# A two-block model on one core: another order of the mixer's branches, three jobs at a time, and other durations in the emission clock

## The chip, the core and the metric

The kernel runs on one core of a Trainium2 chip. The metric is device time in microseconds (us) of one execution, as the median of several runs. On the core, TensorE (PE) does matrix products, VectorE (DVE), ScalarE (ACT) and GpSimd (POOL) do elementwise work, and SyncE (SP) issues most DMAs. Each engine takes its instructions strictly in the order in which the program issued them, so that an instruction that waits holds up all that stands behind it on its engine.

## The reference

The model has 512 tokens of width 1024. The first block has two layers; each is a mixer, a mixture of experts and a gated per-layer embedding. The second block is an attention with forgetting, a convolutional feed-forward part, an HGRN2 recurrence and a second feed-forward part. The change is in the mixer, which has four branches on the same normed input:

```python
h = rms_norm(x, g_mix[i])
a_q, a_k, a_v, s_z, s_x, s_b, s_c, s_dtf, s_dtb, c_q, c_k, c_v, d_uv = split(h @ w_in[i])
o_a = gqa_block_attention(rope(norm(a_q)), rope(norm(a_k)), a_v)          # branch 0
o_b = bidir_ssd(s_z, s_x, s_b, s_c, s_dtf, s_dtb, ...)                     # branch 1
#     depthwise conv of 5 taps, two state-space scans, times silu(z), rms_norm
o_c = rms_norm(diff_block_attention(c_q, c_k, c_v, lam, rel_bias)) * ...   # branch 2
#     two softmaxes per head, subtracted
o_d = spatial_gating(d_uv, ...)                                           # branch 3
gates = sigmoid(h @ w_branch_gate[i])                                     # 1024 -> 4 * 1024
merged = sum_n gates[n] * (branch_n @ w_branch[i][n])                     # 256 -> 1024 each
x = x + merged @ w_out[i]
```

## The kernel before

Activations lie feature by token: eight tiles of 128 x 512. Dense products are made to float32 accuracy from two halves: a weight piece of 128 x 1024 is split by ScalarE into a high half `ph` (a cast) and by VectorE, every fourth time by GpSimd, into a low half `pl` (a subtraction), and each product is three matmuls (high by high, high by low, low by high). An output tile of 128 x 512 from 1024 inputs is thus a *step* of 24 matmuls; a step of a branch's output product (`w_branch`, 256 inputs) has six.

The mixer (`Net.mixer`) runs two things side by side. The **filler** is a list of such steps (`blocks`): the projections by `w_in`, the 32 gate steps with the 32 branch steps in between (`steps`), and `w_out`. `Runner.go` issues it step by step. After a step's matmuls it issues its *evacuation* (VectorE takes the result from PSUM into a tile `w`); there are two PSUM banks `mm` for it. `PCS` weight pieces (four, with their tiles `ph` and `pl`) may be split and not yet used up, and SyncE loads 1 MB blocks of weights into `RAW` = 2 buffers. The **jobs** are Python generators (`jobs`): the norm, the setup, the decay terms of the state-space branch, and the four branches, `gqa` (branch 0), `sgu` (3), `diff` (2), `ssm` (1). After every six filler matmuls, `Runner.go` may issue one job step: `Jobs.step` looks at the first `window` = 2 jobs of the list and takes the first that is due. A branch's output step waits until its job is done; if that isn't so when its turn comes, job steps are issued one after another with no filler between them.

Whether a job is due, and whether one may be issued at all, is told by a model of the engines' times, `Clock`: `Clock.run` adds for each issued instruction an estimated duration to its engine. A job waits until the clock of TensorE has reached the time at which its last results are there, plus `LAG`; and no job step is issued while the clock of VectorE or ScalarE is more than `slack` = 4 us ahead of that of TensorE. The same clock orders the issue of the later phases `fox` and `hgrn` (with `window` = 1) and of `ple`.

In `steps`, the gates come in the order `[3, 0, 2, 1]`, with the projections `z` and `x` of the state-space branch behind the first eight gate steps. A branch's eight output steps follow its gates four steps later, one after each filler step (`behind`). In `jobs`, `diff` waits for `gqa`, and `ssm` waits for all of `x` and for `diff`. The tiles `w` (2 KB a partition) come from a pool of `WN` = 38. In `ssm`, `start` and `taps` are the convolution (its weights are `cwh`), `fetch` loads rows of decay sums over SyncE's queue (`w<-lrow`), `rows` makes the decay matrix `f` and the weights `u.W` of a head (with `col`), `weights` multiplies them, three products of each head on GpSimd, and `outputs` makes the head's output.

Of the kernel before, what the change touches and what calls it, by code (L numbers as in the profile page):

```python
# [13 lines left out]
F32 = mybir.dt.float32  # L14
# [123 lines left out]
class Clock:  # L138


    LAG = 0.15

    def __init__(self):
        self.t = dict.fromkeys(("tensor", "vector", "scalar", "gpsimd", "sync"), 0.0)
# [6 lines left out]
    def run(self, eng, f, out, ins, accum):  # L151
        start = max([self.t[eng], self.free.pop(out.tensor.name, 0.0)] + [self.done.get(a.tensor.name, 0.0) for a in ins])
        n = max([a.free_size() for a in ins] + [out.free_size()])
        if f == "dma_start":
            self.dma = max(self.dma, start) + out.size() / 90000
            cost, busy = self.dma + 2.0 - start, 0.1
        elif eng == "tensor":
            passes = 2 if f == "transpose" else 4 if ins[-1].dtype == F32 else 1
            cost = busy = 0.0025 + passes * ins[-1].free_size() / 2400 * (0.5 if out.shape[0] <= 64 else 1)
        else:  # L160
            fix, per = {"vector": (0.07, 960), "scalar": (0.1, 1200), "gpsimd": (0.15, 476)}[eng]
            cost = busy = fix + n / per
        self.t[eng] = start + busy
        for a in [out] + accum:
            self.done[a.tensor.name] = start + cost + self.LAG
        for a in [out] + ins:
            self.last[a.tensor.name] = start + cost + self.LAG
        if eng != "tensor":
            self.mark = max(self.mark, start + cost + self.LAG)

# [372 lines left out]
class Net:  # L543
# [246 lines left out]
    def mixer(self, i, X, nxt):  # L790
        nc, I = self.nc, self.I
        w = I["w_in"][i]
# [43 lines left out]
        def steps():  # L836

            behind = deque()
            order = [3, 0, 2, 1]
            src = [("g", order[0]), ("p", proj("z", O_Z, 256, 0.5)), ("p", proj("x", O_X, 768))] + [("g", n) for n in order[1:]]  # L840
            for kind, v in src:
                if kind == "g":
                    behind.extend([None] * max(0, 4 - len(behind)))
                    behind.extend(branch(v, v == order[0], v == order[-1]))
                for st in gates(v) if kind == "g" else v:
                    yield st
                    b = behind.popleft() if behind else None
                    if b is not None:
                        yield b
            yield from (b for b in behind if b is not None)  # L850
# [12 lines left out]
        def blocks():  # L863
            yield from proj("aq", O_AQ, 256, cols=qv)
            yield from proj("akv", O_AK, 256)
            yield from proj("uv", O_U, 512, 0.5)
            yield from proj("cq", O_CQ, 256, -(32.0 ** -0.5))
            yield from proj("ck", O_CK, 256)
            yield from proj("cv", O_CV, 256)
            yield from steps()  # L870
            yield Step([], None, turn_over, ready=lambda: len(ms) == ND)
            yield from self.stream(I["w_out"][i], 0, D, ms, evo)
# [9 lines left out]
        def jobs():  # L882
            yield self.xnorm_job(N)
            if i == 0:
                yield chain((lambda: N.R is not None,), self.setup_job(), self.bias_job())
            yield chain((lambda: "setup" in self.made,), self.decays(i, dtw, xs, N, B))
            yield job(0, lambda: self.gqa(i, pj.pop("aq"), pj["akv"], rope), wait("akv", 2), lambda: "setup" in self.made)
            yield job(3, lambda: self.sgu(i, pj.pop("uv")), wait("uv", 4))
            yield job(2, lambda: self.diff(i, pj.pop("cq") + pj.pop("ck"), pj.pop("cv")), wait("cv", 2), lambda: 0 in out)
            yield job(1, lambda: self.ssm(i, B, wait("x", 6), lambda: (pj.pop("z"), pj.pop("x"))), lambda: 2 in out)  # L890

        X.runner = Runner(self, blocks())
        yield
        with self.phase(X, {"mm": 2, "s": 2, "t": 2, "po": 2}, wk=False), ExitStack() as wctx, self.tc.manual_schedule():
            self.wk = wctx.enter_context(self.work(f"m{i}", X.side))
            self.SM, self.WN, self.POOL = "t", 38, 4
            dtw = self.dt_load(w[:, O_DT:O_DT + 8], 8)
            rope = self.rope_load()
            X.runner.go(*jobs(), until=lambda: X.R is not None, slack=4)

    def dt_load(self, wsrc, n):
        rv = self.t(self.wk, [128, ND, n], F32, "dtr", 1)
# [390 lines left out]
        B.dtv, B.col, B.ncol, B.wst, B.lrow = dtv, col, ncol, wst, lrow  # L1293
        yield

    def ssm(self, i, B, ready, get):
        nc, wk = self.nc, self.wk
        dtv, col, ncol, wst, lrow = B.dtv, B.col, B.ncol, B.wst, B.lrow

# [7 lines left out]
            return out  # L1307

        yield ready
        sz, sx = get()  # L1310

        cw, cb = self.cw[i], self.cb[i]
        cx = []
# [69 lines left out]
        def rows(u):  # L1383
            g, r = divmod(u.h, 2)
            G = grp[g]
            if r == 0:
                pg = self.psum("t")
                for c in range(NT):
                    sl = slice(c * 128, (c + 1) * 128)
                    self.mm(pg[:, sl], bf[g][:, sl], cf[g][:, sl])  # L1390
                G.G = self.w2k()
                nc.scalar.copy(G.G, pg)

            f, b = u.M
            for c in range(NT):
                sl = slice(c * 128, (c + 1) * 128)
                nc.scalar.activation(f[:, sl], f[:, sl], AF.Identity, bias=ncol[:, c, u.h:u.h + 1])
            yield
            for c in range(NT):
                sl = slice(c * 128, (c + 1) * 128)  # L1400
                nc.vector.scalar_tensor_tensor(f[:, sl], b[:, sl], col[:, 1, c, u.h:u.h + 1], f[:, sl], op0=OP.subtract, op1=OP.min)
            nc.scalar.activation(f, f, AF.Exp)

            u.W = self.w2k()
            for c in range(NT):
                sl = slice(c * 128, (c + 1) * 128)
                nc.scalar.activation(u.W[:, sl], self.c("le"), AF.Identity, scale=dtv[:, 0, c, u.h:u.h + 1])
# [13 lines left out]
        def outputs(u):  # L1421
# [3 lines left out]
            for c in range(NT):  # L1425
# [5 lines left out]
                if c < NT - 1:  # L1431
                    self.mm(o, cs[c + 1][:, g, 1, r], u.E[1][:, sl], start=False, stop=True)
            if r == 1:
                y = ys[g] = xf[g]
                nc.vector.scalar_tensor_tensor(y, xf[g], self.sm(f"dsk{i}", g), grp[g].py, op0=OP.mult, op1=OP.add)
                t = self.w2k()
# [4 lines left out]
        for n in range(6):  # L1441
            r = rows(H[n]) if n < 4 else None
            if r is not None:
                next(r)
            if n >= 2:
                outputs(H[n - 2])
            yield
# [621 lines left out]
    def hgrn(self, X, nxt):  # L2069
# [22 lines left out]
                    nc.scalar.activation(H[g].b, H[g].b, AF.Ln, scale=co[:, 0, g:g + 1], bias=co[:, 2, g:g + 1])  # L2092

        def silu(ps, tag):
            x, s = tl(tag, 3), tl("w", 4)
            nc.vector.scalar_tensor_tensor(x, ps, 0.5, N.R, op0=OP.mult, op1=OP.mult)
            nc.scalar.activation(s, x, AF.Tanh)
            nc.vector.scalar_tensor_tensor(x, s, 1.0, x, op0=OP.add, op1=OP.mult)
            return x
# [237 lines left out]
def kernel(ctx: ExitStack, tc: tile.TileContext, I, soff, out: bass.AP):  # L2337
# [1 line left out]
    gp = net.nc.gpsimd  # L2339
    X = []  # L2340
    for i in range(2):
        X.append(Ahead(net, f"m{i}", "left", f"g_mix{i}", 28, 4, adder=gp if i else None))
        X.append(AheadMoe(net, f"e{i}", "left", "right", i, 11, 6, 2))
        X.append(Ahead(net, f"p{i}", "right", f"g_ple{i}", 16, 3, adder=gp))
        X[-1].pw = []
# [43 lines left out]
```

## Time and profile before

| | us |
|---|---|
| median of 3 runs | 3509.37 |
| lowest, highest | 3505.4, 3511.45 |
| the profiled execution, its own time | 3513.49 |
| its span, first to last instruction | 3511.7 |

| engine | busy us | share of the span | instructions |
|---|---|---|---|
| PE (matmul) | 3311.0 | 94% | 16658 |
| DVE | 1682.0 | 48% | 2852 |
| ACT | 1118.4 | 32% | 1826 |
| POOL | 309.7 | 9% | 184 |

Rows of the profile name an instruction by what it writes and reads, as `pl<-raw,ph`. Nearly all of them carry line 196 (L196), that of the helper through which every operation is issued, so that a tile's name, not the line, tells which work it is. A busy matmul row is its time in the pipeline; successive matmuls overlap.

### The profile page before, as it was taken

The page shows a single profiled execution, that of the slowest core. Times are in us where ns is not written, and L with a number is a line of the kernel's source. Part 1 is how long each engine was busy: PE and PEld are TensorE (multiplying, and loading weights), DVE is VectorE, ACT ScalarE, POOL GpSimd, SP SyncE. Part 2 cuts the span into 40 slices and gives each one's busy share as a digit, 9 for nine tenths or more (in the row PEclk, how much of TensorE's full clock was granted, in tenths as well). Part 3 has the DMA queues.
Part 4 walks back from the last instruction along what each step waited for, and adds up shares of the span by engine and source line. Part 5 has one row for each costly group of instructions (what it writes and reads, how often), then busy time and mean ns, then how long its engine had stood idle before and what let it go on. Part 6 is the DMA issues. An engine that isn't in the chain of part 4 may idle for free.

```text
span 3511.7 us, 41101 instructions
## 1 busy us (share of the span) xinstructions
PE 3311.0 (94%) x16658; PEld 2356.6 (67%) x16658; DVE 1682.0 (48%) x2852; ACT 1118.4 (32%) x1826; POOL 309.7 (9%) x184
## 2 busy tenths in 40 slices
PE   7999878998999999898998999999999999999998
PEld 5877765443346788676433446787888888878887
DVE  4656753111116656755110115545656567667556
ACT  3444422000014344432000114345434344434333
POOL 0001331000001000332000002211000000000000
PEclk9999988999999999998999999899999999999999
DMA  5242335999993332325999994222222232212332
GB/s 168 85 125 72 102 115 230 415 420 420 410 381 98 101 108 88 100 86 211 392 420 420 411 394 167 82 68 78 84 96 96 90 102 73 68 65 97 98 100 78
DMA packets 264894, 633.53 MB, mean 180 GB/s; under 512 B 20136, under 2 KB 192680, under 8 KB 215296
## 3 DMA queue, kind: packets, MB, share of 16 engines
q1 hardware_dynamic: 249136, 614.58, 47.0%
q10 hardware_dynamic: 15568, 16.32, 1.5%
q8 instruction: 131, 2.15, 0.3%
q14 instruction: 59, 0.48, 0.0%
HBM read 618.15 MB, written 4.31 MB: 177 GB/s over the span
## 4 chain that ended last, share of the span: by engine, by line
PE 72%; DMA 15%; DVE 9%; ACT 2%; issue 2%; POOL 1%; SPq 0%; DVEq 0%; ACTq 0%; POOLq 0%
PE mm L196 58%; DMA xraw<-in_w_exp_down_dram 6%; PE po L196 5%; PE t L196 4%; DMA xraw<-in_w_exp_gate_dram 3%; PE sm L196 3%; DMA xraw<-in_w_exp_up_dram 3%; DVE w L196 3%; DVE pl L196 2%; PE s L196 2%; DVE x L196 1%; DVE ach L196 1%; PE a L196 1%; ACT ph L196 1%; DMA ach<-in_pT_dram 1%
## 5 line engine op out<-in xcount | busy, mean ns | idle before, releaser
L196 PE MATMUL mm<-ach,ph 128*128 128x512 f32 x5504 | 1748.7, 399 | 61.1 <-DVE w L196 36.2
L196 PEld LDWEIGHTS mm<-ach,ph 128*128 128x128 f32 x5504 | 1026.0, 190 | 304.2 <-issue 50.7
L196 PE MATMUL mm<-ach,pl 128*128 128x512 f32 x2752 | 1083.7, 394 | 0.9 <-DVE pl L196 0.8
L196 PEld LDWEIGHTS mm<-ach,pl 128*128 128x128 f32 x2752 | 523.4, 190 | 115.7 <-DVE pl L196 2.9
L196 ACT CAST ph<-raw 128x1024 fp32r<-128x1024 f32 (+1 forms) x366 | 373.3, 1029 | 309.4 <-PE mm L196 271.2
L196 DVE TENSOR_TENSOR pl<-raw,ph 128x1024 fp32r<-128x1024 f32 (+1 forms) x317 | 391.2, 1238 | 113.3 <-ACT ph L196 111.5
L196 PE MATMUL mm<-xraw,xe 128*64 128x512 f32 x1312 | 330.9, 599 | 17.7 <-DMA xraw<-in_w_exp_gate_dram 10.4
L196 PE MATMUL mm<-xraw,hT 128*64 128x512 f32 x928 | 228.5, 595 | 22.3 <-DMA xraw<-in_w_exp_down_dram 21.5
L196 PEld LDWEIGHTS mm<-xraw,xe 128*64 128x64 f32 x1312 | 104.7, 138 | 202.5 <-issue 166.4
L196 POOL TENSOR_TENSOR pl<-raw,ph 128x1024 fp32r<-128x1024 f32 x49 | 119.9, 2446 | 754.6 <-ACT ph L196 718.1
L196 PEld LDWEIGHTS mm<-xraw,hT 128*64 128x64 f32 x928 | 73.0, 137 | 161.1 <-issue 116.9
L196 DVE TENSOR_TENSOR sg<-sg,mm 128x512 f32<-128x512 f32 x32 | 22.0, 688 | 326.5 <-PE mm L196 326.5
L196 ACT ACTIVATE w<-w 128x512 f32<-128x512 f32 x122 | 75.1, 628 | 250.6 <-DVE w L196 247.8
L196 ACT ACTIVATE yy<-mm,ac 128x512 fp32r<-128x512 f32 x32 | 22.0, 687 | 393.6 <-PE mm L196 393.6
L196 DVE SCALAR_TENSOR_TENSOR yy<-mm,ac,yy 128x512 fp32r<-128x512 f32 x32 | 24.0, 750 | 231.5 <-ACT yy L196 230.6
L196 DVE SCALAR_TENSOR_TENSOR y<-u,small,y 128x512 f32<-128x512 f32 x176 | 131.8, 749 | 3.1
L196 POOL TENSOR_TENSOR w<-w,w 128x512 f32<-128x512 f32 x72 | 110.4, 1545 | 250.8 <-DVE w L196 243.8
L196 PE MATMUL mm<-xraw,sqt 128*64 128x512 f32 x448 | 118.3, 606 | 9.3 <-DMA xraw<-in_w_exp_gate_dram 6.6
L196 DVE TENSOR_TENSOR x<-x,sm 128x512 f32<-128x512 f32 x76 | 51.4, 687 | 140.1 <-PE sm L196 140.1
L196 DVE TENSOR_TENSOR w<-mm,R 128x512 f32<-128x512 f32 x92 | 63.2, 688 | 106.0 <-PE mm L196 96.5
L196 ACT ACTIVATE sg<-mm 128x512 f32<-128x512 f32 x32 | 19.1, 597 | 296.3 <-PE mm L196 296.3
L196 DVE TENSOR_TENSOR x<-x,mm 128x512 f32<-128x512 f32 x80 | 54.5, 685 | 122.0 <-PE mm L196 121.9
(315 smaller groups left out, 3479.0 us busy)
## 6 DMA issues: line engine op xcount, KB each, us to landing
xraw<-in_w_exp_down_dram SPq DMA_DIRECT2D x116, 1024.0 KB, 18.7
xraw<-in_w_exp_up_dram SPq DMA_DIRECT2D x112, 1024.0 KB, 19.8
xraw<-in_w_exp_gate_dram SPq DMA_DIRECT2D x108, 1024.0 KB, 19.8
raw<-in_ffn_w_up_dram SPq DMA_DIRECT2D x44, 1024.0 KB, 5.1
raw<-in_w_branch_gate_dram SPq DMA_DIRECT2D x32, 1024.0 KB, 5.3
raw<-in_w_in_dram SPq DMA_DIRECT2D x22, 1024.0 KB, 5.7
raw<-in_w_exp_gate_dram SPq DMA_DIRECT2D x20, 1024.0 KB, 19.8
raw<-in_w_exp_up_dram SPq DMA_DIRECT2D x16, 1024.0 KB, 18.1
```

The lines of the kernel that those rows point to most:

```text
L196: r = g(*a, **kw)
```

## The change

Five things change. (1) `Clock.run` gets other durations and `LAG` 0.2 instead of 0.15. (2) In the mixer, `x` and `z` are projected with the other projections, `x` as steps 5 to 10 and `z` as steps 15 and 16 of 22, and the gates come in the order `[0, 3, 1, 2]`. (3) The jobs come in the order `gqa`, `ssm`, `sgu`, `diff`; `ssm` waits for `x` and for the decay terms, no longer for `diff`, and waits for `z` only before its fourth head (`gate`); the window is three jobs. (4) The mixer has 42 tiles `w` instead of 38 and three weight pieces instead of four; `ssm` puts `u.W` into the tile of `b` instead of a new one. (5) In `hgrn`, the tiles `q` and `g` have four buffers instead of three.

```diff
--- before.py
+++ after.py
@@ -138,7 +138,7 @@
 class Clock:
 
 
-    LAG = 0.15
+    LAG = 0.2
 
     def __init__(self):
         self.t = dict.fromkeys(("tensor", "vector", "scalar", "gpsimd", "sync"), 0.0)
@@ -153,13 +153,20 @@
         n = max([a.free_size() for a in ins] + [out.free_size()])
         if f == "dma_start":
             self.dma = max(self.dma, start) + out.size() / 90000
-            cost, busy = self.dma + 2.0 - start, 0.1
+            cost, busy = self.dma + 2.0 - start, 0.1 if eng == "sync" else 0.45
+        elif f == "transpose":
+            cost = busy = 0.109
         elif eng == "tensor":
-            passes = 2 if f == "transpose" else 4 if ins[-1].dtype == F32 else 1
-            cost = busy = 0.0025 + passes * ins[-1].free_size() / 2400 * (0.5 if out.shape[0] <= 64 else 1)
+
+            n = ins[-1].free_size()
+            if ins[-1].dtype == F32:
+                cost = max(0.224, 0.004 + n / 600) * (0.5 if out.shape[0] <= 64 else 1)
+            else:
+                cost = max(0.112, 0.0134 + n / 2400) * (0.5 if ins[0].shape[0] <= 64 else 1)
+            busy = cost
         else:
-            fix, per = {"vector": (0.07, 960), "scalar": (0.1, 1200), "gpsimd": (0.15, 476)}[eng]
-            cost = busy = fix + n / per
+            fix, per = {"vector": (0.2, 960), "scalar": (0.26, 1270), "gpsimd": (0.2, 466)}[eng]
+            cost = busy = fix + n / per + (0.19 if eng == "scalar" and accum else 0)
         self.t[eng] = start + busy
         for a in [out] + accum:
             self.done[a.tensor.name] = start + cost + self.LAG
@@ -836,8 +843,8 @@
         def steps():
 
             behind = deque()
-            order = [3, 0, 2, 1]
-            src = [("g", order[0]), ("p", proj("z", O_Z, 256, 0.5)), ("p", proj("x", O_X, 768))] + [("g", n) for n in order[1:]]
+            order = [0, 3, 1, 2]
+            src = [("g", n) for n in order]
             for kind, v in src:
                 if kind == "g":
                     behind.extend([None] * max(0, 4 - len(behind)))
@@ -863,7 +870,9 @@
         def blocks():
             yield from proj("aq", O_AQ, 256, cols=qv)
             yield from proj("akv", O_AK, 256)
+            yield from proj("x", O_X, 768)
             yield from proj("uv", O_U, 512, 0.5)
+            yield from proj("z", O_Z, 256, 0.5)
             yield from proj("cq", O_CQ, 256, -(32.0 ** -0.5))
             yield from proj("ck", O_CK, 256)
             yield from proj("cv", O_CV, 256)
@@ -885,18 +894,18 @@
                 yield chain((lambda: N.R is not None,), self.setup_job(), self.bias_job())
             yield chain((lambda: "setup" in self.made,), self.decays(i, dtw, xs, N, B))
             yield job(0, lambda: self.gqa(i, pj.pop("aq"), pj["akv"], rope), wait("akv", 2), lambda: "setup" in self.made)
+            yield job(1, lambda: self.ssm(i, B, wait("x", 6), wait("z", 2), pj.pop), lambda: "lrow" in B.__dict__)
             yield job(3, lambda: self.sgu(i, pj.pop("uv")), wait("uv", 4))
             yield job(2, lambda: self.diff(i, pj.pop("cq") + pj.pop("ck"), pj.pop("cv")), wait("cv", 2), lambda: 0 in out)
-            yield job(1, lambda: self.ssm(i, B, wait("x", 6), lambda: (pj.pop("z"), pj.pop("x"))), lambda: 2 in out)
 
         X.runner = Runner(self, blocks())
         yield
         with self.phase(X, {"mm": 2, "s": 2, "t": 2, "po": 2}, wk=False), ExitStack() as wctx, self.tc.manual_schedule():
             self.wk = wctx.enter_context(self.work(f"m{i}", X.side))
-            self.SM, self.WN, self.POOL = "t", 38, 4
+            self.SM, self.WN, self.POOL = "t", 42, 4
             dtw = self.dt_load(w[:, O_DT:O_DT + 8], 8)
             rope = self.rope_load()
-            X.runner.go(*jobs(), until=lambda: X.R is not None, slack=4)
+            X.runner.go(*jobs(), until=lambda: X.R is not None, slack=4, window=3)
 
     def dt_load(self, wsrc, n):
         rv = self.t(self.wk, [128, ND, n], F32, "dtr", 1)
@@ -1293,7 +1302,7 @@
         B.dtv, B.col, B.ncol, B.wst, B.lrow = dtv, col, ncol, wst, lrow
         yield
 
-    def ssm(self, i, B, ready, get):
+    def ssm(self, i, B, ready, gate, get):
         nc, wk = self.nc, self.wk
         dtv, col, ncol, wst, lrow = B.dtv, B.col, B.ncol, B.wst, B.lrow
 
@@ -1307,7 +1316,7 @@
             return out
 
         yield ready
-        sz, sx = get()
+        sx = get("x")
 
         cw, cb = self.cw[i], self.cb[i]
         cx = []
@@ -1401,7 +1410,7 @@
                 nc.vector.scalar_tensor_tensor(f[:, sl], b[:, sl], col[:, 1, c, u.h:u.h + 1], f[:, sl], op0=OP.subtract, op1=OP.min)
             nc.scalar.activation(f, f, AF.Exp)
 
-            u.W = self.w2k()
+            u.W = b
             for c in range(NT):
                 sl = slice(c * 128, (c + 1) * 128)
                 nc.scalar.activation(u.W[:, sl], self.c("le"), AF.Identity, scale=dtv[:, 0, c, u.h:u.h + 1])
@@ -1431,6 +1440,7 @@
                 if c < NT - 1:
                     self.mm(o, cs[c + 1][:, g, 1, r], u.E[1][:, sl], start=False, stop=True)
             if r == 1:
+                sz = B.sz
                 y = ys[g] = xf[g]
                 nc.vector.scalar_tensor_tensor(y, xf[g], self.sm(f"dsk{i}", g), grp[g].py, op0=OP.mult, op1=OP.add)
                 t = self.w2k()
@@ -1442,6 +1452,9 @@
             r = rows(H[n]) if n < 4 else None
             if r is not None:
                 next(r)
+            if n == 3:
+                yield gate
+                B.sz = get("z")
             if n >= 2:
                 outputs(H[n - 2])
             yield
@@ -2092,7 +2105,7 @@
                     nc.scalar.activation(H[g].b, H[g].b, AF.Ln, scale=co[:, 0, g:g + 1], bias=co[:, 2, g:g + 1])
 
         def silu(ps, tag):
-            x, s = tl(tag, 3), tl("w", 4)
+            x, s = tl(tag, 4), tl("w", 4)
             nc.vector.scalar_tensor_tensor(x, ps, 0.5, N.R, op0=OP.mult, op1=OP.mult)
             nc.scalar.activation(s, x, AF.Tanh)
             nc.vector.scalar_tensor_tensor(x, s, 1.0, x, op0=OP.add, op1=OP.mult)
@@ -2339,7 +2352,7 @@
     gp = net.nc.gpsimd
     X = []
     for i in range(2):
-        X.append(Ahead(net, f"m{i}", "left", f"g_mix{i}", 28, 4, adder=gp if i else None))
+        X.append(Ahead(net, f"m{i}", "left", f"g_mix{i}", 28, 3, adder=gp if i else None))
         X.append(AheadMoe(net, f"e{i}", "left", "right", i, 11, 6, 2))
         X.append(Ahead(net, f"p{i}", "right", f"g_ple{i}", 16, 3, adder=gp))
         X[-1].pw = []
```

## Rows read from the trace of the kernel before

**Rows 1.** Page, part 4: the chain that ended last, shares of the span by engine.
```profile
PE 72%; DMA 15%; DVE 9%; ACT 2%; issue 2%; POOL 1%; SPq 0%; DVEq 0%; ACTq 0%; POOLq 0%
```

**Rows 2.** Windows, first mixer; the first line names the columns.
```profile
core 0: us, PE busy (x) PEld busy (x) DVE busy (x) ACT busy (x) POOL busy (x), PEclk, DMA share, GB/s
110.00:168.00 58.00, 57.91 (x375) 46.97 (x374) 35.11 (x63) 27.29 (x54) 2.86 (x2) 1.00 0.29 85
168.00:220.00 52.00, 51.71 (x303) 41.59 (x301) 26.03 (x50) 24.58 (x46) 4.78 (x2) 1.00 0.41 119
220.00:255.00 35.00, 34.05 (x177) 27.33 (x177) 21.09 (x39) 13.47 (x25) 2.41 (x1) 1.00 0.43 118
255.00:320.00 65.00, 65.00 (x377) 52.43 (x376) 39.86 (x96) 32.89 (x67) 8.23 (x4) 1.00 0.23 73
320.00:400.00 80.00, 72.27 (x334) 58.12 (x333) 60.40 (x83) 29.18 (x42) 21.43 (x12) 0.96 0.23 73
400.00:460.00 60.00, 47.88 (x214) 39.16 (x213) 34.05 (x56) 25.75 (x55) 28.97 (x20) 0.90 0.45 136
460.00:475.00 15.00, 7.67 (x51) 7.11 (x49) 6.71 (x18) 1.49 (x3) 0.77 (x1) 0.73 0.15 52
475.00:507.00 32.00, 28.04 (x114) 22.43 (x114) 16.43 (x17) 8.83 (x13) 10.14 (x6) 0.93 0.20 66
```

**Rows 3.** Windows, second mixer, same columns.
```profile
1150.00:1210.00 60.00, 59.88 (x318) 49.16 (x317) 40.07 (x87) 22.41 (x33) 4.78 (x2) 1.00 0.40 113
1210.00:1300.00 90.00, 89.97 (x576) 72.51 (x576) 47.67 (x80) 45.39 (x91) 4.81 (x2) 1.00 0.29 87
1300.00:1390.00 90.00, 90.00 (x517) 72.93 (x514) 56.91 (x126) 43.95 (x88) 9.61 (x4) 1.00 0.33 98
1390.00:1460.00 70.00, 62.34 (x292) 49.25 (x291) 53.29 (x67) 25.89 (x37) 17.12 (x9) 0.98 0.21 69
1460.00:1545.00 85.00, 75.39 (x365) 60.82 (x364) 56.57 (x99) 31.54 (x64) 35.49 (x24) 0.96 0.35 112
1545.00:1600.00 55.00, 50.50 (x219) 40.38 (x217) 33.20 (x34) 18.27 (x25) 20.65 (x12) 1.00 0.35 117
```

**Rows 4.** Waits of TensorE, 300 to 600: us in total, times, longest.
```profile
PE mm L196 <- DVE w L196: 14.9, 6, 4.5
PE po L196 <- DVE w L196: 9.0, 2, 4.8
```

**Rows 5.** Waits of TensorE, 1380 to 1690, same columns.
```profile
PE mm L196 <- DVE w L196: 17.1, 12, 2.8
```

**Rows 6.** Tile s, 0 to 600: duration min/median/max, first and last start.
```profile
L196 DVE TENSOR_REDUCE st<-s x16: 680/686/693, 134.9 to 176.0; 128x1 f32<-128x512 f32 x16
```

**Rows 7.** Tile w, 0 to 600, same columns.
```profile
L196 SPq DMA_DIRECT2D w<-w x64: 461/582/1724, 100.6 to 245.8; - x64
L196 DVE CUSTOM_DVE_ANT_0 w<-s,th x32: 681/686/693, 209.2 to 302.3; 128x512 f32<-128x512 f32 x32
L196 DVE SCALAR_TENSOR_TENSOR w<-w,col,w x32: 276/312/1403, 394.1 to 443.5; 128x64 f32<-128x64 f32 x16, 128x128 f32<-128x128 f32 x16
L196 DVE SCALAR_TENSOR_TENSOR w<-w,cwh,w x24: 737/750/2911, 332.6 to 376.8; 128x510 f32<-128x510 f32 x12, 128x511 f32<-128x511 f32 x12
```

**Rows 8.** Lines by form, 60 to 560: busy us, mean ns, idle before and its releasers.
```profile
L196 ACT CAST ph<-raw 128x1024 fp32r<-128x1024 f32 x62 | 64.1, 1038 | 27.8 <-PE mm L196 19.6 <-issue 3.5 <-DMA raw<-in_w_in_dram 2.9
L196 DVE TENSOR_TENSOR pl<-raw,ph 128x1024 fp32r<-128x1024 f32 x47 | 59.5, 1266 | 26.3 <-ACT ph L196 26.3
L196 POOL TENSOR_TENSOR w<-w,w 128x512 f32<-128x512 f32 x36 | 54.3, 1519 | 130.8 <-DVE w L196 126.8 <-PE mm L196 4.0
L196 POOL TENSOR_TENSOR pl<-raw,ph 128x1024 fp32r<-128x1024 f32 x15 | 36.9, 2458 | 254.1 <-ACT ph L196 230.2 <-DMA w<-w 23.9
L196 DVE SCALAR_TENSOR_TENSOR w<-w,st,w 128x512 f32<-128x512 f32 x16 | 12.6, 785 | 0.6
L196 DVE SCALAR_TENSOR_TENSOR w<-w,cwh,w 128x510 f32<-128x510 f32 x12 | 14.5, 1206 | 6.9 <-ACT w L196 6.7
L196 DVE SCALAR_TENSOR_TENSOR w<-w,col,w 128x128 f32<-128x128 f32 x16 | 10.7, 728 | 2.4 <-ACT w L196 2.4
```

**Rows 9.** The chain in order of time, one undisturbed stretch: start, us, what.
```profile
1302.23 17.71 PE mm L196 x78
```

**Rows 10.** Windows in the two later attention-like phases, columns as in rows 2.
```profile
2200.00:2250.00 50.00, 44.24 (x213) 36.39 (x212) 28.32 (x62) 17.07 (x26) 10.93 (x5) 0.83 0.22 65
2950.00:3000.00 50.00, 50.00 (x333) 44.76 (x332) 33.60 (x69) 20.45 (x30) 0.00 (x0) 1.00 0.20 64
```

**Rows 11.** Windows at the end of the first mixer and in the experts, same columns.
```profile
540.00:550.00 10.00, 10.00 (x40) 6.41 (x38) 2.08 (x3) 0.65 (x2) 0.00 (x0) 1.00 0.00 0
650.00:700.00 50.00, 50.00 (x268) 22.21 (x266) 5.64 (x8) 3.56 (x6) 0.00 (x0) 1.00 1.01 420
```

## The prediction

> **What bounds the kernel now.** I read the page's chain first, then busy time stage by stage, and then what TensorE waits for where it is not busy. The chain that ended last is 72% TensorE and 15% DMA [rows 1]; the DMA part is the expert weights, which come in at 420 GB/s with the DMA engines full [rows 11]. The change leaves the experts alone. Their loads stand still in the last stretch of the mixer, with their buffers full, and go on when it is over [rows 11], so that a mixer that ends earlier moves all that follows by the same time. The question is thus how much time TensorE loses in the two mixers.
>
> In both, the reader is to see two halves. In the first half TensorE is practically full: 58 us of 58, 52 of 52, 65 of 65 in the first mixer, with `gqa`, `sgu` and `diff` beside it, and 60 of 60, 90 of 90, 90 of 90 in the second [rows 2, 3]. `diff` alone lies from 209 to 302 [rows 7], and there the idle time is 0 to 1 us in 65 or 35. The second half begins with the convolution of `ssm` at 333 [rows 7], and from there TensorE idles: in the first mixer 80 - 72.27 = 7.7, 60 - 47.88 = 12.1, 15 - 7.67 = 7.3 and 32 - 28.04 = 4.0 us; in the second 70 - 62.34 = 7.7, 85 - 75.39 = 9.6 and 55 - 50.50 = 4.5 us [rows 2, 3]. What TensorE waits for there is VectorE, at `mm` (a PSUM bank that is not evacuated yet) and at `po` (the outputs of `ssm`) [rows 4, 5]. VectorE itself is busy 75 and 76% while the convolution runs, against 50 to 67% in the full stretches. So the kernel is TensorE-bound but for the state-space branch, which is alone at the end of a mixer, with little filler left.
>
> **The change part by part.**
>
> *Removed stalls.* With `ssm` begun after the tenth projection instead of after `diff`, the convolution falls beside plain projections. A filler step there is 24 matmuls; 78 take 17.71 us [rows 9], 0.227 each, so a step is 5.45 us and a branch step of six is 1.36 us. Before, the convolution ran where gate and branch steps alternate: with two `mm` banks, an evacuation must be done within 1.36 us plus what job matmuls lie between, or TensorE stands. Beside projections it has 5.45 us. The stalls of the convolution (7.7 + 7.7) and of the heads and the end of `ssm` (12.1 + 7.3 + 9.6) come to 44.4 us. The last part of each mixer (4.0 + 4.5 us) I keep: the last branch's sum, its split and `w_out` follow one another whichever branch is last.
>
> *Clock.* The granted clock is 1.00 in the full stretches and 0.96, 0.90, 0.73, 0.93 and 0.98, 0.96 where TensorE idled before [rows 2, 3]. Busy time times what is missing gives 2.9 + 4.8 + 2.1 + 2.0 + 1.2 + 3.0 = 16 us if all slow time fell on busy time, 0 if it all fell on the pauses. I take half, 8 us.
>
> *Does VectorE carry it?* Its work stays the same. Over 110 to 475 it is busy 223.3 us of 365, 61%; over 1150 to 1545 it is 254.5 of 395, 64% [rows 2, 3]. TensorE lost nothing at 61 and 63% and 0.1 us in 60 at 67% (1150 to 1210), and 10% at 75%. Spread evenly, the work fits. Spread badly, it would give back what it gains (a rival below).
>
> *The new last branch.* `diff` is now at the end and may leave TensorE waiting as `ssm` did. Bounds: 0, as in the rows of `diff` itself, and 12.1 + 7.3 in each mixer, 39 us, if it ends as `ssm` ended. The stretches that hold `diff` lost at most 1 us, so I stay near 0 and take 11 us.
>
> *Emission clock.* The new figures are nearer to the rows: for 512 elements VectorE goes from 0.60 to 0.73 us (rows: 0.68 to 0.75), GpSimd from 1.23 to 1.30, and a 1024 subtraction on VectorE from 1.14 to 1.27 (row: 1.27) [rows 6 to 8]. With the old ones, a backlog of 4 us by the clock was about 4.8 us in truth. This helps to keep the stalls out that I have already counted; I add nothing. It also reorders the later phases. There TensorE is full in `hgrn` and lost 5.8 us at the worst place of `fox` [rows 10]: 0, within 6 us either way.
>
> *DMA queue.* `fetch` moves forward on SyncE's queue, among weight loads and the small copies of `gqa` and `diff`. Those 64 copies took 0.58 us each, between 100 and 246 [rows 7], with TensorE full. 16 fetches more at that price are 9 us of a queue that has slack: 0. Bound: a weight load behind 24 copies (14 us) against the 10.9 us that a 1 MB block feeds, 3 us, twice in each mixer: 12 us.
>
> *Fewer pieces, more tiles, `u.W` in `b`, four `q` and `g`.* The first is a rival below. `u.W` waits for the readers of `b`, for which the exponential ahead of it on ScalarE waits as well: 0. `hgrn` has no idle time for the fourth buffer to remove [rows 10]: 0.
>
> *A port that VectorE and GpSimd share.* While GpSimd was busy 21 us of 80 and 29 of 60 [rows 2], the 510-wide taps took 1.21 us on average against a median of 0.75, up to 2.9, and the 128-wide `col` operations 0.73 against 0.31 [rows 7, 8]: 12 x 0.46 + 16 x 0.42 = 12 us of VectorE in a mixer. The Trainium skill, "SBUF — State Buffer", section "SBUF: two separate sides", says that a VectorE operation with two SBUF inputs and a GpSimd operation that reads SBUF exclude each other for a whole instruction; the long taps agree. By that rule the 16 subtractions of `diff` (`w<-w,st,w`), now beside GpSimd's adds of `merged`, could each meet one; by the rows they took 0.785 us with GpSimd busy 8.2 us of 65, hardly over a tap's median, and I leave the sum as it is.
>
> **Sum.** 44.4 + 8 - 11 = 41 us. The profiled execution took 3513.5 us; 3513.5 - 41 = 3472.5. The median of the runs is 4.1 us below that execution: 3468 us. At best, with all 16 us of clock and half of the 8.5 us kept, 44.4 + 16 + 4 = 64: 3445.
>
> **Rivals.**
>
> *`gqa` is late or `diff` ends badly.* The branch of `gqa` is now wanted after 26 steps (142 us of filler) instead of 34 and 8 branch steps (196 us), and `gqa` shares VectorE with `ssm`. For it: its last score lay at 176 [rows 6], and a wait of up to 4 us for VectorE at some 16 steps moves that by tens of us. Against it: issued without filler, its eight ticks cost TensorE little, some two reductions of 0.69 each; 8 x 1.4 x 2 mixers = 22 us. That gives 3490. If instead `diff` costs the whole 39 us, 28 more than I took, 3496. Both together, or VectorE at 76% over a third of each mixer (10% of 120 us, twice, 24 us) on top, make it 3510 to 3520: no change.
>
> *Three weight pieces are too few (slower).* Where gate and branch steps alternate, a new piece takes the tiles of the one three before: from the end of that one to its own use lie 1.36 + 5.45 + 1.36 = 8.2 us, against 15 with four. A cast and a subtraction take 1.04 + 1.27 or, on GpSimd, 1.04 + 2.46 us [rows 8]; with the permitted 4 us of VectorE's backlog ahead 6.3, with two adds of 1.5 ahead on GpSimd 6.5. It fits, but half of it is gone if the subtraction is issued half a step late. There were 62 casts from 60 to 560 [rows 8], so 124 pieces in two mixers. From 48 / 124 = 0.39 us lost for each piece on, the kernel is slower than before; at 0.5 us it is 62 us, 3530. Against it: in rows 4 and 5 the waits are for `w`, not for `pl`.
>
> *The lock.* GpSimd's adds meet every one of those 16 operations for a whole add, 16 x 1.52 x 2 = 49 us, all of it in TensorE's way: 3517. This is the rule of the page above, carried to its end; the rows speak for less.
>
> *Nothing changes,* since the same stalls come elsewhere: 3509.
>
> **How the numbers follow.** My forecast (3444 to 3488) gets 0.66, the first rival (3488 to 3512, a few us beyond) 0.20, three pieces 0.09, the lock 0.03, nothing 0.02. 0.2% is 7 us. Faster: 0.66 and 0.12 of the first rival, 0.78. Same: its other 0.08 and 0.02, 0.10. Slower: 0.12. The range 3440 to 3505 leaves out the three last cases and some 0.06 of the first rival.
>
> **What would show it.** Right: the taps (`w<-w,cwh,w`) begin near 100 in the first mixer, not at 333, beside a full TensorE, and take nearer to 0.75 us on average; `diff`'s `w<-s,th` is the last job; no 50 us stretch of the mixers before the last 40 has over 2 us idle; `w_out` begins about 25 us earlier in the first mixer and 40 us earlier in the second. Wrong: waits of `mm` for `pl`; `po` of `gqa` issued in a row without `mm` between, and TensorE waiting there for `st` or `w`; VectorE above 75% between 100 and 250; or a longer `fox`.

## The result and the profile after

The changed kernel takes 3486.9 us (median of five runs), before 3509.0: ratio 0.9939, interval 0.9925 to 0.9954, 22 us or 0.6% faster. One of the five executions took 11526 us, its 128x512 matmuls 1.10 us on average instead of 0.40; the ratio leaves it out, and the profile shown is of a second series (`e1_after`), which gave 3485.8 us, ratio 0.9932 (0.9920 to 0.9944). The forecast was 41 us.

First the windows of the first mixer in the changed kernel, the stretches of rows 2; behind the stretch's length stands TensorE's busy time.

```profile
110.00:168.00 58.00, 58.00 (x323) 47.49 (x322) 45.15 (x76) 29.28 (x53) 4.58 (x2) 1.00 0.32 96
168.00:220.00 52.00, 51.97 (x346) 42.32 (x346) 30.64 (x62) 26.58 (x49) 5.12 (x2) 1.00 0.21 62
220.00:255.00 35.00, 34.90 (x182) 28.25 (x181) 23.77 (x39) 20.11 (x45) 13.88 (x9) 1.00 0.60 171
255.00:320.00 65.00, 56.32 (x290) 45.88 (x289) 38.20 (x79) 24.73 (x46) 12.13 (x8) 0.95 0.33 100
320.00:400.00 80.00, 78.64 (x417) 63.21 (x416) 54.25 (x98) 36.53 (x72) 21.50 (x13) 1.00 0.35 104
400.00:460.00 60.00, 60.00 (x321) 48.87 (x320) 31.34 (x57) 21.95 (x35) 15.65 (x9) 1.00 0.27 88
460.00:475.00 15.00, 12.25 (x53) 9.43 (x53) 11.38 (x12) 5.59 (x9) 7.22 (x5) 1.00 0.21 71
475.00:507.00 32.00, 30.98 (x125) 21.99 (x124) 15.70 (x17) 9.10 (x12) 7.34 (x4) 1.00 0.60 230
```

The reader is to see where the pauses went. 320 to 475, which lost 27.2 us [rows 2], now loses 1.4 + 0 + 2.8, with the granted clock at 1.00. New is 255 to 320 with 8.7 us. Over 110 to 507 TensorE idles 13.9 us instead of 32.5. VectorE is busiest in 110 to 168, 45.15 of 58 us or 78%, and TensorE loses nothing there. Next, tile `w` from 0 to 560, durations and first and last start:

```profile
L203 DVE CUSTOM_DVE_ANT_0 w<-s,th x32: 677/684/692, 282.4 to 410.1; 128x512 f32<-128x512 f32 x32
L203 DVE SCALAR_TENSOR_TENSOR w<-w,cwh,w x24: 740/750/2293, 97.7 to 187.2; 128x510 f32<-128x510 f32 x12, 128x511 f32<-128x511 f32 x12
```

The taps begin at 98 instead of 333, and `diff` is the last job, its scores from 282 to 410, 73 us ahead of the first write of `w_out` (482.7). TensorE's waits at `mm` for `w` from 300 to 560 fall from 14.9 us to 3.7 [rows 4], from 0 to 560 from 17.8 to 7.7; in the second mixer they fall from 18.5 (1120 to 1600) to 11.1 (1080 to 1600):

```profile
PE mm L203 <- DVE w L203: 3.7, 3, 1.5
```

Where a mixer ends is told by the last write of `x` behind `w_out`. Before, and after, first and second mixer (the last number of the range is the end):

```profile
L196 DVE SCALAR_TENSOR_TENSOR x<-mm,x x8: 691/692/692, 517.2 to 562.5; 128x512 f32<-128x512 f32 x8
L196 DVE SCALAR_TENSOR_TENSOR x<-mm,x x8: 691/692/692, 1594.7 to 1640.0; 128x512 f32<-128x512 f32 x8
```

```profile
L203 DVE SCALAR_TENSOR_TENSOR x<-mm,x x8: 684/692/692, 482.7 to 527.4; 128x512 f32<-128x512 f32 x8
L203 DVE SCALAR_TENSOR_TENSOR x<-mm,x x8: 684/692/692, 1546.6 to 1591.3; 128x512 f32<-128x512 f32 x8
```

The first mixer ends 35.1 us earlier, the second 48.7. The embedding phase between lies 37.6 us earlier, so the second mixer itself gained 48.7 - 37.6 = 11.1. The mixers together gained 46.2 us, more than the 41 forecast; and at the start of `fox` the changed kernel is 50.8 us ahead (the last write of `x` in the second embedding phase is at 2153.0 instead of 2203.8). At the end it is 27.8 us ahead by the spans of these two executions (the one of before lies 4.5 us above its median; by the medians the gain is 22). **Some 24 us are lost again in phases for which the prediction put nothing.** They are lost by the end of `hgrn`. Here are its last gate projection (`g<-mm,R`) and its last head's output (`o`), before and after:

```profile
L196 DVE SCALAR_TENSOR_TENSOR g<-mm,R x8: 683/688/692, 2885.5 to 3066.6; 128x512 f32<-128x512 f32 x8
```

```profile
L196 DVE SCALAR_TENSOR_TENSOR o<-o,small,g x8: 751/752/753, 2922.4 to 3104.5; 128x512 f32<-128x512 f32 x8
```

```profile
L203 DVE SCALAR_TENSOR_TENSOR g<-mm,R x8: 683/684/692, 2843.6 to 3020.5; 128x512 f32<-128x512 f32 x8
```

```profile
L203 DVE SCALAR_TENSOR_TENSOR o<-o,small,g x8: 751/752/753, 2893.2 to 3078.1; 128x512 f32<-128x512 f32 x8
```

Before, the last head was done 3104.5 - 3066.6 = 37.9 us behind the last projection; after, 3078.1 - 3020.5 = 57.6. In that tail only the output product is left as filler, and TensorE idles 8 us in one window at a granted clock of 0.90; before, it was full there. The window of the tail before, then two of after:

```profile
3050.00:3100.00 50.00, 50.00 (x302) 43.44 (x301) 31.88 (x63) 15.78 (x27) 0.00 (x0) 1.00 0.21 66
```

```profile
2950.00:3000.00 50.00, 50.00 (x306) 44.31 (x305) 34.70 (x63) 21.88 (x33) 0.00 (x0) 1.00 0.23 74
3000.00:3050.00 50.00, 42.03 (x245) 35.91 (x245) 32.14 (x71) 13.58 (x24) 0.00 (x0) 0.90 0.10 32
```

### The profile page after: what moved, and what is told of

It reads as the page before. It is cut to its first block, busy times and chain, and to the rows that moved or that the text cites. A ratio compares the mean times of both kernels' runs of the same rounds, so it can differ in the third digit from the quotient of the medians.

```text
span 11524.7 us, 41090 instructions
## 1 busy us (share of the span) xinstructions
PE 11474.2 (100%) x16658; PEld 5479.3 (48%) x16658; DVE 1659.6 (14%) x2852; ACT 1147.2 (10%) x1826; POOL 299.6 (3%) x184
## 4 chain that ended last, share of the span: by engine, by line
PE 99%; DVE 0%; DMA 0%; issue 0%; ACT 0%; DVEq 0%; ACTq 0%
PE mm L203 84%; PE po L203 5%; PE sm L203 4%; PE t L203 4%; PE s L203 2%; PE a L203 1%; PE u L203 0%; DVE rt L203 0%; DVE m L203 0%; DMA raw<-in_w_in_dram 0%; DVE x L203 0%; DMA small<-in_small_dram 0%; DVE ac L203 0%; DVE xe L203 0%; ACT ph L203 0%
## 5 line engine op out<-in xcount | busy, mean ns | idle before, releaser
L203 PE MATMUL mm<-ach,ph 128*128 128x512 f32 x5504 | 5297.2, 1098 | 19.0 <-ACT ph L203 14.8
L203 PEld LDWEIGHTS mm<-ach,ph 128*128 128x128 f32 x5504 | 2344.2, 430 | 2106.8 <-issue 2042.6
L203 PE MATMUL mm<-ach,pl 128*128 128x512 f32 x2752 | 3007.8, 1093 | 0.0
L203 PEld LDWEIGHTS mm<-ach,pl 128*128 128x128 f32 x2752 | 1157.6, 421 | 1063.9 <-issue 1050.1
L203 PE MATMUL mm<-xraw,xe 128*64 128x512 f32 x1312 | 1188.0, 1924 | 0.0
L203 PE MATMUL mm<-xraw,hT 128*64 128x512 f32 x928 | 819.4, 1925 | 0.0
L203 PE MATMUL mm<-xraw,sqt 128*64 128x512 f32 x448 | 402.9, 1929 | 0.0
L203 PE MATMUL mm<-raw,xe 128*64 128x512 f32 x224 | 291.2, 1916 | 0.0
L203 PE MATMUL mm<-ph,ach 128*128 128x256 f32 x512 | 288.3, 675 | 0.0
L203 PEld LDWEIGHTS mm<-ph,ach 128*128 128x128 f32 x512 | 249.3, 556 | 13.9 <-issue 12.4
```

The lines of the kernel that those rows point to most:

```text
L203: r = g(*a, **kw)
```

## The experiments

Each kernel is timed against the kernel before on the same chip; ratios are to it.

**e1_after: the changed kernel, for its trace.**

> The changed kernel itself, for a trace: about 3487 us. Theory A (the stalls of the state-space branch go, some come back at the end of diff): idle time of TensorE in the first mixer falls from 31 to under 12 us between the first projection and w_out, and what is left lies in its last 100 us. Theory B (VectorE is only crowded earlier): 10 us or more of idle time lie between 100 and 250. Theory C (three pieces): the waits at mm are for pl or ph, 10 us or more in all. Theory D (the later phases got longer by the new clock): the mixers save 40 us, and fox, hgrn or ple lose 15 to 20.

3485.8 us. Theory D, and A in part: idle time in the first mixer is 13.9 us, a little over A's 12, and 8.7 of it lie in 255 to 320 and not in the last 100 us, where A had it. It is not in 110 to 250 (0.1 us up to 255), so B falls; the waits at `mm` are for `w`, so C has nothing to show; the loss lies behind the mixers.

**e2_order_old_clock: the change without its clock.**

```diff
-    LAG = 0.2            # and the durations of Clock.run as before
+    LAG = 0.15
```

> The change without its new clock: durations and LAG of the kernel before, order, jobs, window, tiles and pieces of the changed one. If the order does the work (theory A), 3475 to 3500 us, within 10 of the changed kernel. If the clock does it, 3500 or more. If the new clock harms the later phases (theory D), it is faster than the changed kernel by 10 us or more.

3469.6 us, ratio 0.9893 (0.9878 to 0.9907): 16 us *faster* than the changed kernel. The mixers end at 535.9 and 1603.1, a gain of 26.6 and 8.0 us for order, window, tiles and pieces. The new clock as a whole costs time.

**e3_clock_in_mixers: the new clock in the mixers alone.**

```diff
             self.SM, self.WN, self.POOL = "t", 42, 4
+            self.clock.new, self.clock.LAG = True, 0.2
...
             X.runner.go(*jobs(), until=lambda: X.R is not None, slack=4, window=3)
+            self.clock.new, self.clock.LAG = False, 0.15
```

> The changed kernel, with the clock of before in all that follows a mixer. Theory D: 3465 to 3477 us, 10 to 20 below the changed kernel. Otherwise within 4 us of it.

3459.0 us, ratio 0.9855 (0.9842 to 0.9868), **50 us faster than before and 27 faster than the changed kernel**; the best version of this study. Theory D holds and its price is higher than I had put it. Against e2 the clock gains in the mixers: they end at 527.8 instead of 535.9, and the second one, counted from the phase before it, takes 500.7 instead of 506.0 us. So the new durations save 13 us by these marks (11 by the medians) in the mixers, and lose 27 behind them. In `hgrn` the tail is back at 3053.5 - 3015.6 = 37.9 us and the window full:

```profile
L214 DVE SCALAR_TENSOR_TENSOR g<-mm,R x8: 682/688/692, 2834.5 to 3015.6; 128x512 f32<-128x512 f32 x8
```

```profile
L214 DVE SCALAR_TENSOR_TENSOR o<-o,small,g x8: 752/752/753, 2871.4 to 3053.5; 128x512 f32<-128x512 f32 x8
```

```profile
3000.00:3050.00 50.00, 50.00 (x297) 43.27 (x297) 32.58 (x67) 15.62 (x26) 0.00 (x0) 1.00 0.20 66
```

**e4_before_three_pieces: three weight pieces in the kernel before.**

```diff
-        X.append(Ahead(net, f"m{i}", "left", f"g_mix{i}", 28, 4, ...))
+        X.append(Ahead(net, f"m{i}", "left", f"g_mix{i}", 28, 3, ...))
```

> The kernel before with three weight pieces in the mixers instead of four, nothing else. Theory C: 10 us or more slower than before, 3520 us up, with TensorE waiting for pl or ph in the mixers. Otherwise 3505 to 3515.

3495.7 us, ratio 0.9962 (0.9948 to 0.9975): faster, which no theory expected. By the marks the mixers gain 1.2 and 3.3 us of it. Most of the rest lies in the first experts' phase with its embedding (559.0 us instead of 563.5) and in the last feed-forward phase (394.9 instead of 399.0), whose source is untouched; why is open. That three pieces are too few is refuted for the kernel before; in the changed one, which was not run with four, the mixers show no waits at `mm` for `pl`.

**e5 to e7: which phase, which durations.** e5 uses the old clock in `hgrn` alone; e6 and e7 split the durations behind the mixers.

```diff
-        if self.new:                                      # in Clock.run: new durations
+        if self.new or eng == "tensor" or f == "dma_start":     # e6
+        if self.new or eng != "tensor" and f != "dma_start":    # e7, with LAG 0.2
```

> The changed kernel with the clock of before during hgrn alone. Theory D1 (most of the 27 us that the later phases lose is hgrn's, 16 by its stretch of the trace, the rest fox's): 3465 to 3473 us. Rival (it is spread over ple and the experts' end too, or fox has most of it): 3476 or more.

3471.8 us, ratio 0.9893 (0.9877 to 0.9910): half of the loss, 14 of 27 us, is `hgrn`'s: within D1's range, though hardly "most". At the start of `fox` the changed kernel has 9.0 us idle at a granted clock of 0.76, the e3 kernel 6.2 us at 0.90:

```profile
2150.00:2200.00 50.00, 41.05 (x182) 33.25 (x181) 26.89 (x49) 13.75 (x20) 10.88 (x5) 0.76 0.22 65
```

```profile
2150.00:2200.00 50.00, 43.85 (x228) 36.52 (x226) 29.98 (x67) 18.06 (x27) 10.95 (x5) 0.90 0.21 65
```

What TensorE waits for there in the changed kernel, 2150 to 2500, is the first projection's operand `dtw` (6.6 us instead of 3.5 in e3) and the first probabilities `pT` (no such wait in e3):

```profile
PE t L203 <- DVE dtw L203: 6.6, 1, 6.6
PE po L203 <- ACT pT L203: 3.7, 3, 1.9
```

> Behind the mixers, TensorE and the DMAs by the new durations, the elementwise engines and LAG by those of before. Theory E (the longer elementwise durations make a pipe's tick due later): about 3459 us, as with the whole old clock there. Rival (TensorE's new durations change how the filler is counted against the jobs): 3475 or more.

3467.2 us, ratio 0.9880 (0.9865 to 0.9895): 8 us above e3, between the two expectations.

> Behind the mixers, the elementwise engines and LAG by the new durations, TensorE and the DMAs by those of before. Theory E: 3485 us or more, since the ticks come due late and TensorE's clock runs a little slower as well. Rival: 3465 or less.

3486.7 us, ratio 0.9935 (0.9920 to 0.9949): the elementwise durations and `LAG` alone bring the whole loss back. Theory E holds for the larger part; the two halves, 28 and 8 us, do not add up to the 27 of both. Elementwise durations and `LAG` were not tried apart.

**e8 and e9: the new clock, with jobs due earlier.**

```diff
-            if not force and job.due > self.net.clock.now or ...:
+            if not force and job.due > self.net.clock.now + self.early or ...:
...
-            X.runner.go(self.xnorm_job(X), pipe, ..., window=1)
+            X.runner.go(self.xnorm_job(X), pipe, ..., window=1, early=4.0)    # e9: 2.0; fox likewise
```

> The changed kernel with its new clock everywhere; in fox and hgrn alone a job counts as due 4 us before its results are there by the clock. Theory E (the clock is right, but a tick need not be complete before the next one is issued): 3458 to 3468 us, hgrn back to about 253 us from its first load to its last. Rival (a tick issued too early makes TensorE wait for it): 3486 or more.

3501.4 us, ratio 0.9977 (0.9966 to 0.9988): the rival. `hgrn`'s tail did shrink, to 29.9 us, but TensorE now waits at each of the eight ticks for a head's tile `i` (waits in `hgrn`: total, times, longest):

```profile
PE a L203 <- DVE i L203: 13.3, 8, 2.1
```

The tail is 27.7 us shorter than in the changed kernel, and the stretch from the first to the last `g` 27.4 us longer (204.3 instead of 176.9), so that `fox` and `hgrn` together gain nothing (924.3 against 925.1 us). So the marks don't show them as what makes e8 slower than the changed kernel: in this profiled execution, the fastest of ten at 3491.5 us, 8.2 us more lie in the last feed-forward phase, and where the other nine lose more is not known.

> The changed kernel with its new clock everywhere; in fox and hgrn a job counts as due 2 us early instead of 4. Theory F (two prices against each other: late ticks lengthen hgrn's tail, early ticks make TensorE wait at each of them): between the two, a tail of 35 to 45 us and under 5 us of waits for the tile i, 3465 to 3478 us. Rival (any fixed lead is worse than the changed kernel): 3487 or more.

3468.8 us, ratio 0.9882 (0.9865 to 0.9899), tail 35.1 us, and no wait for `i`; the two longest waits are:

```profile
PE sm L203 <- DVE sqa L203: 2.9, 1, 2.9
PE mm L203 <- DVE x L203: 2.0, 4, 0.8
```

So there are two prices against each other, and a lead of 2 us does better than none or 4. That the old, too short durations acted as such a lead fits e7, but was not tried by itself. All kernels with this change side by side, in us: from the last write of `x` in the second embedding phase to the end of `hgrn`; from the same write to the first product of probabilities in `fox` (`po<-pT,v`); in `hgrn` from the first to the last `g`; and the tail, from the last `g` to the last `o`.

| | `fox` to `hgrn`'s end | to `fox`'s first `po` | first to last `g` | tail |
|---|---|---|---|---|
| before | 900.7 | 67.4 | 181.1 | 37.9 |
| changed (e1) | 925.1 | 78.9 | 176.9 | 57.6 |
| e2, old clock | 900.6 | 67.3 | 181.1 | 37.9 |
| e3, new in the mixers | 898.0 | 64.9 | 181.1 | 37.9 |
| e5, old in `hgrn` | 907.5 | 77.0 | 181.1 | 37.9 |
| e6, TensorE and DMA new | 905.4 | 70.3 | 187.0 | 33.8 |
| e7, elementwise and `LAG` new | 926.7 | 78.2 | 182.3 | 59.3 |
| e8, 4 us early | 924.3 | 68.6 | 204.3 | 29.9 |
| e9, 2 us early | 901.8 | 69.0 | 182.0 | 35.1 |

Where the elementwise durations are new and there is no lead, `fox`'s pipe starts 77 to 79 us into the phase instead of 65 to 70, and, but for e5 with its old clock there, `hgrn`'s tail is 58 to 59 us long.

**e10 and e11: what in the order does it.**

```diff
-            yield from proj("x", O_X, 768)                 # e10, on e3; z likewise
+            src = [("g", order[0]), ("p", proj("z", ...)), ("p", proj("x", ...))] + [...]
```

> The clock-in-mixers kernel (3459 us), but x and z projected where the kernel before had them, behind eight gate steps, and jobs, window and gate order as in the change. Theory A1 (the gain comes from the convolution falling beside plain projections): the convolution starts near 200 in the first mixer and 3475 us or more. Rival (it is enough that the state-space branch runs beside the others and not alone at the end): 3455 to 3467 us.

3547.5 us, ratio 1.0110 (1.0088 to 1.0132), 88 us slower than e3. The taps begin at 268, `ssm` is still third to be wanted, and its branch holds up the filler (waits of TensorE, 60 to 560):

```profile
PE po L214 <- DVE w L214: 27.9, 3, 18.3
PE mm L214 <- DVE w L214: 10.9, 7, 2.6
```

e11 is the kernel before with the state-space branch set free:

```diff
...                                                  # three pieces, 42 tiles, u.W in b
-            yield job(1, lambda: self.ssm(...), lambda: 2 in out)
+            yield job(1, lambda: self.ssm(...), lambda: "lrow" in B.__dict__)
-            X.runner.go(*jobs(), until=..., slack=4)
+            X.runner.go(*jobs(), until=..., slack=4, window=3)
```

> The kernel before with its clock, its projections, its gate order and its order of jobs, with three pieces, 42 tiles, u.W in b, a window of three jobs, and the state-space branch waiting for the decay terms instead of for diff. Theory A1: about the kernel before with three pieces alone, 3485 to 3500 us. Rival: 3475 or less.

3489.1 us, ratio 0.9946 (0.9925 to 0.9967), 7 us under e4, with intervals that overlap. Its first mixer ends 16 us before e4's (545.3, 561.3), its second takes 8.1 us more (518.8, 510.7). Running the branch beside others helps little without the early projection. How much of e10's loss is the place of the convolution and how much the early turn of its branch, e10 does not tell apart.

**e12_two_pieces: e3 with two weight pieces.**

```diff
-        X.append(Ahead(net, f"m{i}", "left", f"g_mix{i}", 28, 3, ...))
+        X.append(Ahead(net, f"m{i}", "left", f"g_mix{i}", 28, 2, ...))
```

> The clock-in-mixers kernel with two weight pieces in the mixers instead of three. If pieces were near their limit at three, TensorE now waits for ph or pl: 60 matmul steps and 30 branch steps a mixer at 0.5 us or more, 3500 us up. If the waits for the evacuation set the pace and fewer pieces only lighten VectorE's queue ahead, as three against four in the kernel before seemed to: 3465 or less.

3662.6 us, ratio 1.0434 (1.0413 to 1.0454), 204 us above e3. The limit that I feared for three pieces stands at two; the waits of TensorE, 60 to 560, are of the kind that the rival named:

```profile
PE mm L214 <- ACT ph L214: 30.4, 24, 3.1
PE mm L214 <- DVE pl L214: 19.4, 23, 2.5
PE mm L214 <- POOL pl L214: 17.4, 8, 4.7
```

## Why the prediction was right, and where its sum was wrong

- **The convolution beside projections: right.** It runs from 98 to 187 beside a full TensorE (58.0 of 58 and 52.0 of 52 us). VectorE above 75% between 100 and 250 stood among the signs of being wrong; it came, 78% in 110 to 168, and cost nothing, while 75% beside gate and branch steps had cost 10% [rows 2]. e10, which takes the early projection away, is 88 us slower, though part of that may come from the early turn of the branch.
- **44.4 us of stalls, 11 of them back, 8 us of granted clock: near for the mixers, in part by luck.** They gained 46.2 us, in the first more than forecast (35 instead of about 25), in the second less (11 instead of 16). Windows over the first mixer and over the second, before and after:

```profile
17.00:562.00 545.00, 506.05 (x2557) 402.45 (x2556) 310.91 (x562) 206.90 (x368) 95.83 (x53) 0.96 0.33 100
1126.00:1640.00 514.00, 489.25 (x2535) 387.70 (x2535) 310.54 (x529) 202.88 (x357) 97.24 (x53) 0.99 0.32 100
```

```profile
17.00:527.00 510.00, 494.00 (x2559) 392.62 (x2557) 305.36 (x563) 207.40 (x368) 95.44 (x53) 0.99 0.35 107
1088.40:1591.30 502.90, 485.11 (x2535) 386.17 (x2535) 298.53 (x528) 202.21 (x357) 94.80 (x53) 1.00 0.33 102
```

  Idle time falls by 23.0 and 7.0 us, 30 against the 44.4 - 11 = 33 of the sum. Busy time falls by 12.1 and 4.1 us for practically the same matmuls, at a higher granted clock: 16 us, the upper bound of the clock term, of which the sum took half. And without the new durations (e2) the mixers gain only 34.6 us, less than the 41 forecast; the rest is from a term that the prediction put at nothing.
- **The pauses that stay: wrong place.** I had them behind `diff`; there are 3.8 us in 460 to 507. Most lie where `ssm` ends and `diff` begins, 8.7 us in 255 to 320 and 90 - 82.89 = 7.1 in the second mixer (the 4.5 in 1510 to 1560 are what the sum kept for its end), so the sign that no 50 us would lose over 2 us failed:

```profile
1260.00:1350.00 90.00, 82.89 (x431) 67.71 (x430) 51.67 (x100) 36.09 (x71) 23.86 (x15) 0.98 0.40 119
1350.00:1420.00 70.00, 68.06 (x346) 54.44 (x346) 45.33 (x84) 32.33 (x62) 16.12 (x9) 1.00 0.41 123
1420.00:1510.00 90.00, 87.75 (x479) 69.89 (x480) 56.09 (x103) 38.58 (x71) 23.25 (x13) 1.00 0.23 74
1510.00:1560.00 50.00, 45.55 (x191) 34.64 (x190) 26.92 (x29) 16.54 (x23) 16.65 (x10) 1.00 0.49 178
```

  The chain in the first mixer runs there through the load of `diff`'s first bias table (`th`), five small copies of which two are shown, and VectorE; that `diff` starts late for its own loads is read from this chain, not tried:

```profile
261.65 5.63 DMA th<-rbias
...
267.30 0.51 SPq L203
...
269.76 0.59 SPq L203
...
270.39 1.98 DMA w<-w
...
272.42 0.69 DVE w L203
```

- **The step that failed: "It also reorders the later phases. [...] 0, within 6 us either way."** Measured: 27 us (e1 against e3). That the time still fell into the range, which reaches to 3505, is due to its width: the gain is half of the forecast. I argued from phases that had no idle time to lose. But a job that becomes due later makes no pause where it is delayed; in `hgrn` it moves its work to the end, where the filler is gone. e7 puts it to the elementwise durations and `LAG`, e5 half of it to `hgrn`, e8 and e9 show the two prices. In `fox`, whose getting longer stood among the signs of being wrong, the loss goes with a pipe that starts 10 to 14 us late (e1, e5 and e7 in the table against before and e3); why it starts late was not tried.
- **The clock in the mixers: "I add nothing".** It gains 11 us there (e2 against e3). That this is because `slack` ties the durations there to a backlog is my reading; no run tries it.
- **Four buffers for `q` and `g`: 0, right.** e2, which has them, takes 900.6 us from `fox` to `hgrn`'s end, before 900.7. The 42 tiles and `u.W` in `b` were not tried alone.
- **Three pieces too few: wrong at three, right at two.**
- **`gqa` late:** its last score is at 184.6 instead of 176.0, and the filler was not held up; the rival didn't come.
- **The lock: right that it moves, small.** Lines by form, 60 to 560:

```profile
L203 DVE SCALAR_TENSOR_TENSOR w<-w,st,w 128x512 f32<-128x512 f32 x16 | 19.9, 1241 | 0.6
L203 DVE SCALAR_TENSOR_TENSOR w<-w,cwh,w 128x510 f32<-128x510 f32 x12 | 10.5, 878 | 8.0 <-ACT w L203 7.8
L203 DVE SCALAR_TENSOR_TENSOR w<-w,col,w 128x128 f32<-128x128 f32 x16 | 6.6, 475 | 0.0
```

  The 510-wide taps fell from 1.21 to 0.88 us and the `col` operations from 0.73 to 0.48; `diff`'s `w<-w,st,w` rose from 0.785 to 1.241 us, 16 x 0.456 = 7.3 us of VectorE, not the 24 of the extreme. The Trainium skill, "SBUF — State Buffer", section "SBUF: two separate sides", has it that a VectorE operation with two SBUF inputs and a GpSimd operation that reads SBUF shut each other out for a whole instruction; the trace agrees. Seven of the sixteen `w<-w,st,w` meet no GpSimd operation and take 0.75 us; the other nine overlap an add or a subtraction of GpSimd and take 1.27 to 2.88. Before, one of sixteen did, with 1.28 us. So not every one met an add, as the extreme had it, but more than half met one. One that meets none and one that does, in the changed kernel (start, us, what):

```profile
380.73 0.75 DVE L203 SCALAR_TENSOR_TENSOR w<-w,st,w 128x512 f32<-128x512 f32 x1
```

```profile
388.33 1.29 POOL L203 TENSOR_TENSOR w<-w,w 128x512 f32<-128x512 f32 x1 [10.93 <-DVE rs L203]
388.68 1.49 DVE L203 SCALAR_TENSOR_TENSOR w<-w,st,w 128x512 f32<-128x512 f32 x1
```

## What to carry to other kernels

Put the job that loads VectorE most beside filler whose results may be fetched late, not where banks must be free within a short step, and give it its inputs first. A planner's durations and its rule for "due" are one setting: here truer durations helped the phases that also bound the backlog and hurt those that only wait for a job to be complete, though that the bound is what decides was not tried. When a shared planner is changed, measure each phase that uses it by itself; here leaving the others alone more than doubled the gain, 50 us instead of 22.

## What was not expected

Fewer weight pieces made the kernel before faster by 13 us (e4), only 4.5 of them in the mixers. And the last feed-forward phase, from `hgrn`'s last `o` to the first store, takes 392 to 406 us in these kernels (397.7 in the changed one, 399.0 before, 405.9 in e8, 392.2 in e7), though its source is the same in all: a difference of this size in that phase should not be read as an effect of an edit. This is also why the table above stops at the end of `hgrn`.
